# Products of 512 moving columns in the mLSTM (keys with values, gates of two heads) and in part of the last down projection, on one core

## The chip, the cores and the metric

The kernel runs on one core of a Trainium2 chip. The metric is the device time of one execution in microseconds (us). Engines are named as the profile names them: PE is TensorE's matmul (PEld its weight load), DVE is VectorE, ACT ScalarE, POOL GpSimd, SP the engine that issues most DMAs.

## The reference

A trunk of two layers runs over 640 tokens (512 of a prompt, 8 times 16 of a sample batch), model width 1024, all in 32-bit floats. In each layer one input projection feeds three mixers (a linear recurrence, an mLSTM with four heads of width 256, and windowed attention); their outputs are projected, gated, merged and projected again, and an MLP of width 4096 follows. What the change touches, cut to what matters:

```
u = rms_norm(x, norm1_g)
z = u @ w_in                     # (xa, ga, mq, mk, mv, mo, mi, mf, ...) = split(z)
k_m = mk * M_HEAD_DIM ** -0.5    # keys; q_m = mq, v_m = mv; 4 heads of 256 columns each
# per chunk: w = (q k^T) * exp(log_d - m_t);  num = w v + inter_w * (q C)
#            C_new = decay * C + sum_s wk_s k_s v_s^T     (C: 256 x 256 per head and sequence)
y_b = (rms_norm(h_m) * sigmoid(mo)) @ w_ob
...
x = x + square(relu(rms_norm(x, norm2_g) @ w_up)) @ w_down
```

The prompt is one sequence. The sample batch is eight sequences, each with its own stored C of 256 x 256 per head, which is read, used and written back.

## The kernel before

**Products.** Each 32-bit operand is split into a high part that TensorE takes in its fast 32-bit format (type fp32r) and a low rest. A product is three passes: high times high, low times high, high times low. Weights come in jobs of 1024 rows by 256 columns, in one fixed list (`jobs`). `prep` loads half a job into one of two raw buffers (`wraw`), casts the high part on ACT (L142) and subtracts on DVE for the low part (L143); a pair `whi`, `wlo` holds 256 rows, so that a job fills four pairs of six buffers each. `next_w` prepares one job ahead.

`gemm_w` (L167) holds the weights still and moves 320 token columns. `gemm_x` (L185) holds 128 tokens still and moves 256 weight columns: five blocks of tokens (t = 0 to 4) one after the other, each with 24 matmuls, so that a block's result leaves as soon as it is done, while the next is computed.

**Accumulators.** PSUM has eight banks of 512 floats a partition. `ps_acc` gives one of two tiles of two banks (`acc`), which only the big products use. `ps_small` gives one of four tiles of one bank (`psb`), which everything else shares.

**The mLSTM** (L408 and on). For each head the program writes down: keys by `gemm_x`, queries by `gemm_w`, values by `gemm_x`, output gates by `gemm_x`; transposes of the keys (L507, L510); then the head's recurrence over five blocks of tokens, each with scores (L538), a product with the values (L545), with the carried state (L548) and an update of it (L552). In the fifth block `sample` takes the eight stored states. For each sequence it loads C into one of five `cb` buffers (L451), splits it (`ch` on ACT L455, `cl` on DVE L456), multiplies it with the queries (L459, four matmuls that gather in one of two `psb` tiles kept for four sequences each), forms the update from `kvs` (L463, two matmuls, each into a `psb` tile), adds it on DVE (L465) and stores C (L467). The head ends with a chain of small DVE operations (L572 to L579), five scalings (L581) and ten transposes (L587, L590). While this goes on the block's own result (`pn`) keeps a third `psb` tile.

**What sets the order.** The engines take their instructions in the order of their own queues, and that order is fixed when the program is built. A scheduler chooses it by a simulation of its own: an instruction that stands earlier in the source goes first when its inputs and its buffer are there, and a later one fills in where it is not. So in the program before the products of the next head fill PE between the recurrence's steps. SP issues the DMAs in order too: where one waits for a buffer, those behind it wait.

**The last down projection** (L1179 to L1186) runs `gemm_x` four times with 256 output columns each and adds on DVE (L1181); the outputs leave by DMA.

## Time and profile before

| | us |
|---|---|
| median of three runs | 2929.08 (2927.71 to 2935.36) |
| profiled execution | 2926.99 |
| its span (first to last instruction) | 2925.1 |
| PE busy in it | 2881.9 (99%) |
| DVE, ACT, POOL busy | 1539.6, 1144.9, 304.2 |
| matmuls of `gemm_w`: 13440 of 320 columns (L167) | 1397.2 + 717.3 busy |
| matmuls of `gemm_x`: 4560 of 256 or 264 columns (L185) | 410.6 + 217.4 busy |

Busy time of PE counts a matmul from start to end, and matmuls overlap; how fast they follow each other is read from their starts in the timeline. The mLSTM of the two layers lies at 470 to 840 us and at 1930 to 2300 us of the span.

### The profile page before, as it was taken

To read this page: it belongs to the slowest core of one execution; us is meant where nothing else is said; L and a number is where in the kernel's file an instruction comes from. 1 tells how busy PE (TensorE), PEld (TensorE's weight loads), DVE (VectorE), ACT (ScalarE), POOL (GpSimd) and SP (SyncE) were. 2 spreads that over 40 slices of the span, in tenths; PEclk is the share of its full clock that TensorE was granted. 3 is DMA by queue.
4 is the path that set the end of the run, shared out by engine and by line. 5 is a ranking of instruction groups with operands and counts; after the bars stand their busy time and mean duration, and the time that the engine had idled before them with its cause. 6 is when DMAs were issued, how large, how long until landed. Compare 5 with 4: busy or idle time off the path is not lost.

```text
span 2925.1 us, 50762 instructions
## 1 busy us (share of the span) xinstructions
PE 2881.9 (99%) x20518; PEld 2849.7 (97%) x20518; DVE 1539.6 (53%) x3074; ACT 1144.9 (39%) x2295; POOL 304.2 (10%) x377
## 2 busy tenths in 40 slices
PE   8999999999999999999999999999999999999999
PEld 8999999999999999999999999999999999999999
DVE  7967675444553443333479666655454635333332
ACT  5754444333432332232358444433333323232222
POOL 0210000110112011010012100010111120110110
PEclk9999999999999999999999999999999999999999
DMA  5232224444573322222332322234444733222222
GB/s 172 68 118 80 78 81 118 142 132 134 158 262 108 109 74 83 75 72 73 104 88 68 117 83 80 89 110 146 138 148 139 250 119 100 73 73 73 80 79 73
DMA packets 291210, 319.52 MB, mean 109 GB/s; under 512 B 26424, under 2 KB 259688, under 8 KB 290944
## 3 DMA queue, kind: packets, MB, share of 16 engines
q1 hardware_dynamic: 281440, 300.03, 33.4%
q10 hardware_dynamic: 9536, 16.26, 1.5%
q8 instruction: 161, 2.64, 0.4%
q14 instruction: 73, 0.60, 0.1%
HBM read 255.76 MB, written 62.04 MB: 109 GB/s over the span
## 4 chain that ended last, share of the span: by engine, by line
PE 90%; DVE 4%; DMA 3%; ACT 2%; issue 1%; SPq 0%; POOL 0%; DVEq 0%; ACTq 0%; POOLq 0%
PE acc L167 63%; PE acc L185 16%; DMA out_C_s<-cb 2%; PE psb L743 2%; PE psb L713 1%; PE psb L552 1%; PE psb L735 1%; PE psb L1014 1%; PE psb L548 1%; DVE wlo L143 1%; DMA cb<-in_state_mlstm_C 1%; PE psb L459 1%; PE psb L538 1%; PE psb L545 1%; PE psb L803 0%
## 5 line engine op out<-in xcount | busy, mean ns | idle before, releaser
L167 PE MATMUL acc<-at,whi 128*128 128x320 f32 x8960 | 1397.2, 310 | 1.7 <-DVE xq L972 0.8
L167 PEld LDWEIGHTS acc<-at,whi 128*128 128x128 f32 x8960 | 1330.4, 188 | 3.9 <-issue 1.2
L167 PE MATMUL acc<-at,wlo 128*128 128x320 f32 x4480 | 717.3, 310 | 0.0
L167 PEld LDWEIGHTS acc<-at,wlo 128*128 128x128 f32 x4480 | 670.4, 188 | 0.8
L142 ACT CAST whi<-wraw 128x512 fp32r<-128x512 f32 (+1 forms) x712 | 425.8, 620 | 573.4 <-PE acc L167 496.9
L143 DVE TENSOR_TENSOR wlo<-wraw,whi 128x512 fp32r<-128x512 f32 (+1 forms) x712 | 468.9, 702 | 264.5 <-ACT whi L142 183.0
L185 PE MATMUL acc<-whi,at 128*128 128x256 f32 (+1 forms) x3040 | 410.6, 285 | 14.7 <-ACT vt L499 4.5
L185 PEld LDWEIGHTS acc<-whi,at 128*128 128x128 f32 x3040 | 380.5, 190 | 19.6 <-ACT vt L499 6.0
L185 PE MATMUL acc<-wlo,at 128*128 128x256 f32 (+1 forms) x1520 | 217.4, 282 | 0.0
L185 PEld LDWEIGHTS acc<-wlo,at 128*128 128x128 f32 x1520 | 196.0, 188 | 0.1
L1153 POOL TENSOR_TENSOR ha<-ha 128x640 f32<-128x640 f32 x64 | 82.0, 1281 | 824.4 <-DVE ha L1152 824.4
L1161 DVE TENSOR_TENSOR x<-x,acc 128x640 f32<-128x640 f32 x56 | 45.8, 818 | 153.2 <-PE acc L167 153.2
L116 DVE TENSOR_TENSOR at<-ha,at 128x640 fp32r<-128x640 f32 x64 | 52.8, 825 | 135.1 <-ACT at L115 135.1
L1151 ACT ACTIVATE ha<-acc 128x640 f32<-128x640 f32 x64 | 45.2, 706 | 188.6 <-PE acc L167 188.6
L1152 DVE TENSOR_TENSOR ha<-ha,rbc 128x640 f32<-128x640 f32 x64 | 52.8, 825 | 109.9 <-ACT ha L1151 109.9
L455 ACT CAST ch<-cb 128x516 fp32r<-128x516 f32 x64 | 39.6, 623 | 107.0 <-DMA cb<-in_state_mlstm_C 64.0
L115 ACT CAST at<-ha 128x640 fp32r<-128x640 f32 x64 | 46.6, 728 | 75.0 <-POOL ha L1153 74.3
L465 DVE SCALAR_TENSOR_TENSOR cb<-cb,decb,psb 128x258 f32<-128x258 f32 x128 | 58.1, 478 | 21.3 <-PE psb L463 21.1
L882 ACT ACTIVATE sg<-sg,cvh 128x640 f32<-128x640 f32 x48 | 40.0, 833 | 71.3 <-DVE sg L881 71.3
L691 ACT ACTIVATE prob<-psb,ssm 128x192 f32<-128x192 f32 (+2 forms) x128 | 49.6, 406 | 39.9 <-DVE ssm L689 39.9
L483 POOL TENSOR_SCALAR mo<-mo 128x256 f32<-128x256 f32 x40 | 39.3, 984 | 234.6 <-ACT mo L482 234.6
L456 DVE TENSOR_TENSOR cl<-cb,ch 128x516 fp32r<-128x516 f32 x64 | 43.8, 694 | 29.5 <-ACT ch L455 29.4
(332 smaller groups left out, 2587.3 us busy)
## 6 DMA issues: line engine op xcount, KB each, us to landing
wraw<-in_w_in SPq DMA_DIRECT2D x160, 512.0 KB
wraw<-in_w_up SPq DMA_DIRECT2D x64, 512.0 KB
wraw<-in_w_down SPq DMA_DIRECT2D x64, 512.0 KB
cb<-in_state_mlstm_C SPq DMA_DIRECT2D x64, 256.0 KB
out_C_s<-cb SPq DMA_DIRECT2D x64, 256.0 KB
gdr<-sg ACTq DMA_DIRECT2D x32, 320.0 KB
rl<-ydr SPq DMA_DIRECT2D x32, 320.0 KB
sg<-gdr SPq DMA_DIRECT2D x32, 320.0 KB
```

What stands on the lines that cost most here:

```text
L115: act.copy(dst[:, 0], src)
L116: dve.tensor_tensor(dst[:, 1], src, dst[:, 0].bitcast(F32), ALU.subtract)
L142: act.copy(hi[:, :, :n], r)
L143: dve.tensor_tensor(lo[:, :, :n], r, hi[:, :, :n].bitcast(F32), ALU.subtract)
L167: pe.matmul(acc[:, s, 0:320], lhs, xs[k][:, part, 320 * s:320 * s + 320], start=(i == 0 and k == 0 and part == 0), stop=(i == 1 and k == 7),)
L185: pe.matmul(o, xs[k][:, part, 128 * t:128 * t + 128], wt[:, k % KQ, 0:n], start=(i == 0 and k == 0 and part == 0), stop=(i == 1 and k == 7),)
L465: dve.scalar_tensor_tensor(cb[:, kt, :], cb[:, kt, :], decb[:, h, 4 + b:5 + b], ps[:, 0:258], op0=ALU.mult, op1=ALU.add)
L691: act.activation(o, s, AF.Exp, bias=nm[:, i:i + 1], accum_out=sums[:, i:i + 1])
L743: pe.matmul(po[:, 256 * i:256 * i + 256], vd[:, G - 1 + kb, g].rearrange("p a d -> p (a d)"), pTs[i][:, 256 * kb:256 * kb + 256], start=(k ...
L1152: dve.tensor_tensor(a, a, rbc, ALU.mult)
L1153: pool.tensor_tensor(a, a, a, ALU.mult)
L1161: dve.tensor_tensor(halves(xs[k]), halves(xs[k]), acc[:, :, 0:320], ALU.add)
```

## The change

Two jobs of 256 columns become one of 512, for the keys and values of each head, for the output gates of heads 0 and 1 and of heads 2 and 3, and for the first two of the four jobs of the last down projection. A new function `gemm_xw` computes such a job: it walks over the eight blocks of 128 weight rows, and within each over the five blocks of tokens, into five accumulators that all stay open to the end of the job. Four of them are the two `acc` tiles, the fifth is a `psb` tile. `prep` cuts such a job into four pieces of 256 rows, each loaded by two DMAs, and into eight pairs `whi`, `wlo` of 128 rows, which take turns in the same six buffers. The gates of two heads are computed with the first of them, and the values now directly with the keys.

```diff
@@ -132,6 +132,22 @@
     def prep(j, *hfs):
         ap, n = jobs[j]
         out = ready.setdefault(j, [])
+        if n == 512:
+
+            for q4 in range(4):
+                raw = wp.tile([128, 4, 264], F32, name="wraw", tag="wraw", bufs=2)
+                raw = raw.rearrange("p k c -> p (k c)")[:, 0:1024].rearrange("p (k c) -> p k c", k=2)
+                for i, a in enumerate(ap):
+                    wlast[0] = sp.dma_start(raw[:, :, 256 * i:256 * i + 256],
+                                            a[256 * q4:256 * q4 + 256, :].rearrange("(k p) c -> p k c", p=128))
+                for q in range(2):
+                    hi = wp.tile([128, KQ, 264], F32R, name="whi", tag="whi", bufs=6)
+                    lo = wp.tile([128, KQ, 264], F32R, name="wlo", tag="wlo", bufs=6)
+                    hi, lo = [w.rearrange("p k c -> p (k c)")[:, 0:512] for w in (hi, lo)]
+                    act.copy(hi, raw[:, q])
+                    dve.tensor_tensor(lo, raw[:, q], hi.bitcast(F32), ALU.subtract)
+                    out.append((hi, lo))
+            return
         for hf in hfs or (0, 1):
             raw = wp.tile([128, 4, 264], F32, name="wraw", tag="wraw", bufs=2)
             wlast[0] = sp.dma_start(raw[:, :, :n], ap[512 * hf:512 * hf + 512, :].rearrange("(k p) c -> p k c", p=128))
@@ -188,13 +204,32 @@
                         )
             evac(t, o)
 
+    def gemm_xw(xs, evac):
+
+        w = next_w()
+        a, b, c = ps_acc(), ps_acc(), ps_small()
+        os = [a[:, 0], a[:, 1], b[:, 0], b[:, 1], c]
+        for k in range(8):
+            for t in range(5):
+                x = [xs[k][:, part, 128 * t:128 * t + 128] for part in range(2)]
+                pe.matmul(os[t], x[1], w[k][0], start=(k == 0), stop=False)
+                pe.matmul(os[t], x[0], w[k][0], start=False, stop=False)
+                pe.matmul(os[t], x[0], w[k][1], start=False, stop=(k == 7))
+                if k == 7:
+                    evac(t, os[t])
+
     for l in range(depth):
         win = I["w_in"][l]
 
         def cols(c, n=256):
             return (win[:, c:c + n], n)
 
-        seq = [[cols(c + 256 * h) for c in (C_MK, C_MQ, C_MV, C_MO)] for h in range(4)]
+        def pair(a, b):
+            return ([win[:, a:a + 256], win[:, b:b + 256]], 512)
+
+        seq = [[pair(C_MK + 256 * h, C_MV + 256 * h), cols(C_MQ + 256 * h)] for h in range(4)]
+        for h in (0, 2):
+            seq[h].append(pair(C_MO + 256 * h, C_MO + 256 * h + 256))
         ga = [cols(C_G[0] + 256 * j) for j in range(4)]
         gb = [cols(C_G[1] + 256 * j) for j in range(4)]
         gc = [cols(C_G[2] + 256 * j) for j in range(4)]
@@ -216,7 +251,10 @@
         jobs += ow
         for g in range(4):
             jobs += [(I["w_up"][l][:, 1024 * g + 256 * j:1024 * g + 256 * j + 256], 256) for j in range(4)]
-            jobs += [(I["w_down"][l][1024 * g:1024 * g + 1024, 256 * j:256 * j + 256], 256) for j in range(4)]
+            dn = [(I["w_down"][l][1024 * g:1024 * g + 1024, 256 * j:256 * j + 256], 256) for j in range(4)]
+            if l == depth - 1 and g == 3:
+                dn[0:2] = [([dn[0][0], dn[1][0]], 512)]
+            jobs += dn
 
 
     ssum = [None]
@@ -475,31 +513,31 @@
 
         for h in range(4):
             ktok, qT, vt = wide("ktok", [128, 5, 256]), wide("qT", [128, 2, NT]), wide("vt", [128, 5, 258])
-            mo = wide("mo", [128, 5, 256])
+            if h % 2 == 0:
+                mos = [wide("mo", [128, 5, 256]) for _ in range(2)]
+            mo = mos[h % 2]
             kT, dd, qs = big("kT", [128, 2, NT], 1), big("dmat", [128, 5, 128], 1), big("qs", [128, 2, 384], 1)
 
             def ev_mo(t, o):
-                act.activation(mo[:, t, :], o, AF.Tanh, scale=rth[:, t:t + 1])
-                pool.tensor_scalar(mo[:, t, :], mo[:, t, :], 1.0, None, op0=ALU.add)
-
-
-            def ev_k(t, o):
-                act.activation(ktok[:, t, :], o, AF.Copy, scale=rt16[:, t:t + 1])
-
-            gemm_x(u, ev_k)
+                for i, mo_ in enumerate(mos):
+                    act.activation(mo_[:, t, :], o[:, 256 * i:256 * i + 256], AF.Tanh, scale=rth[:, t:t + 1])
+                    pool.tensor_scalar(mo_[:, t, :], mo_[:, t, :], 1.0, None, op0=ALU.add)
+
+            pool.memset(vt[:, :, 256:257], 1.0)
+            pool.memset(vt[:, :, 257:258], 0.0)
+
+            def ev_kv(t, o):
+                act.activation(ktok[:, t, :], o[:, 0:256], AF.Copy, scale=rt16[:, t:t + 1])
+                act.activation(vt[:, t, 0:256], o[:, 256:512], AF.Copy, scale=rtok[:, t:t + 1])
+
+            gemm_xw(u, ev_kv)
 
             def ev_q(m, acc):
                 dve.tensor_tensor(halves(qT[:, m, :]), acc[:, :, 0:320], halves(rbc), ALU.mult)
 
             gemm_w(u, ev_q)
-            pool.memset(vt[:, :, 256:257], 1.0)
-            pool.memset(vt[:, :, 257:258], 0.0)
-
-            def ev_v(t, o):
-                act.activation(vt[:, t, 0:256], o, AF.Copy, scale=rtok[:, t:t + 1])
-
-            gemm_x(u, ev_v)
-            gemm_x(u, ev_mo)
+            if h % 2 == 0:
+                gemm_xw(u, ev_mo)
 
             for kt in range(2):
                 ps = ps_small()
@@ -1177,13 +1215,13 @@
                     act.copy(yt[t][:, 512 * q4:512 * q4 + 512], ps)
 
             def ev_y(t, o):
-                c = slice(256 * j, 256 * j + 256)
+                c = slice(256 * j, 256 * j + (512 if j == 0 else 256))
                 dve.tensor_tensor(yt[t][:, c], yt[t][:, c], o, ALU.add)
                 dst = O["y_p"][0, 128 * t:128 * t + 128, c] if t < 4 else O["y_s"].rearrange("b s d -> (b s) d")[:, c]
                 sp.dma_start(dst, yt[t][:, c])
 
-            for j in range(4):
-                gemm_x(hid, ev_y)
+            for j in (0, 2, 3):
+                (gemm_x if j else gemm_xw)(hid, ev_y)
 
 
 
```

In the new program the lines behind 134 move: L459 becomes L497, L463 L501, L545 L583, L587 and L590 become L625 and L628, L465 L503, L451 L489, L467 L505; `gemm_xw` is L215 to L217.

PE where the sample part of head 0 begins in layer 0, the program before (`qm` are the queries, `ch` and `cl` the split state, `kvs` the operands of the update):

```order
L545 MATMUL psb<-vt,pt 128x257
L459 MATMUL psb<-ch,qm 128x258
L459 MATMUL psb<-cl,qm 128x258
L459 MATMUL psb<-ch,qm 128x258
L459 MATMUL psb<-cl,qm 128x258
L463 MATMUL psb<-kvs_5412 128x258 x2
L459 MATMUL psb<-ch,qm 128x258
L459 MATMUL psb<-cl,qm 128x258
L459 MATMUL psb<-ch,qm 128x258
L459 MATMUL psb<-cl,qm 128x258
L185 MATMUL acc<-whi,at 128x256 x16
L185 MATMUL acc<-wlo,at 128x256 x3
```

PE at the same place in the program after:

```order
L217 MATMUL acc<-wlo,at 128x512
L583 MATMUL psb<-vt,pt 128x257
L497 MATMUL psb<-ch,qm 128x258
L497 MATMUL psb<-cl,qm 128x258
L497 MATMUL psb<-ch,qm 128x258
L497 MATMUL psb<-cl,qm 128x258
L501 MATMUL psb<-kvs_5436 128x258 x2
L497 MATMUL psb<-ch,qm 128x258
L497 MATMUL psb<-cl,qm 128x258
L497 MATMUL psb<-ch,qm 128x258
L497 MATMUL psb<-cl,qm 128x258
L497 MATMUL psb<-ch,qm 128x258
```

Before, products of the next head stand between the eight sequences from the third on. After, the 48 matmuls of the sample part follow each other with none of the big products among them; the same holds for heads 0, 1 and 2 of both layers, and not for head 3, whose sample part has products of `gemm_w` in between.

PE where the same head ends, the program before (`num` is the head's result, transposed):

```order
L185 MATMUL acc<-whi,at 128x256 x9
L587 MATMUL psb<-cs,num 128x128
L185 MATMUL acc<-whi,at 128x256 x3
L587 MATMUL psb<-cs,num 128x128
L185 MATMUL acc<-whi,at 128x256 x2
L587 MATMUL psb<-cs,num 128x128
L185 MATMUL acc<-whi,at 128x256 x2
L185 MATMUL acc<-wlo,at 128x256
L587 MATMUL psb<-cs,num 128x128
```

PE at the same place in the program after:

```order
L497 MATMUL psb<-ch,qm 128x258
L497 MATMUL psb<-cl,qm 128x258
L501 MATMUL psb<-kvs_5437 128x258 x2
L625 MATMUL psb<-cs,num 128x128 x4
L628 MATMUL psb<-cs,num 128x128
L625 MATMUL psb<-cs,num 128x128 x4
L628 MATMUL psb<-cs,num 128x128
L215 MATMUL psb<-whi,at 128x512
L216 MATMUL psb<-whi,at 128x512
L217 MATMUL psb<-wlo,at 128x512
```

The ten transposes now follow the sample part directly. Behind them come the products of the fifth block of tokens of head 1's keys and values, which are the first to write the job's fifth accumulator (a `psb` tile): 72 of that job's 120 matmuls, those of the other four blocks of tokens for the first six blocks of weight rows, stand ahead of the sample part.

## Rows read from the trace of the kernel before

**Rows 1.** The page, busy time: engine, us (share of the span), instructions

```profile
PE 2881.9 (99%) x20518; PEld 2849.7 (97%) x20518; DVE 1539.6 (53%) x3074; ACT 1144.9 (39%) x2295; POOL 304.2 (10%) x377
```

**Rows 2.** Waits of PE over the span: us in total, times, longest

```profile
PE psb L587 <- DVE num L581: 5.2, 3, 3.6
PE acc L185 <- ACT vt L499: 4.5, 7, 2.0
...
PE psb L463 <- DVE cb L465: 3.5, 5, 1.1
PE acc L185 <- ACT ktok L487: 3.4, 2, 1.7
...
PE psb L459 <- ACT ch L455: 2.6, 4, 1.0
...
PE acc L185 <- DVE qT L492: 1.2, 3, 0.5
```

**Rows 3.** Timeline of PE, last down projection: start, us, engine, line, operation

```profile
2892.96 2.06 PE L185 MATMUL acc<-whi,at 128*128 128x256 f32 x16
2894.86 1.11 PE L185 MATMUL acc<-wlo,at 128*128 128x256 f32 x8
2895.80 2.05 PE L185 MATMUL acc<-whi,at 128*128 128x256 f32 x16
```

**Rows 4.** Timeline of PE, a stretch of `gemm_w`

```profile
888.76 4.85 PE L167 MATMUL acc<-at,whi 128*128 128x320 f32 x32
893.45 2.53 PE L167 MATMUL acc<-at,wlo 128*128 128x320 f32 x16
895.82 4.88 PE L167 MATMUL acc<-at,whi 128*128 128x320 f32 x32
```

**Rows 5.** Stretches from first L459 to last L590, heads 0 to 2, both layers

```profile
core 0: us, PE busy (x) PEld busy (x) DVE busy (x) ACT busy (x) POOL busy (x), PEclk, DMA share, GB/s
549.34:591.30 41.96, 40.09 (x305) 38.97 (x304) 28.62 (x81) 17.27 (x38) 3.67 (x10) 1.00 0.57 170
...
sum 244.34, PE 226.31 PEld 219.02 DVE 167.77 ACT 97.14 POOL 20.33; mean PE 37.72 PEld 36.50 DVE 27.96 ACT 16.19 POOL 3.39
```

**Rows 6.** Timeline of PE, sample part of head 0

```profile
549.77 0.28 PE L459 MATMUL psb<-ch,qm 128*128 128x258 f32 x1
549.88 0.28 PE L459 MATMUL psb<-cl,qm 128*128 128x258 f32 x1
550.00 0.40 PE L463 MATMUL psb<-kvs 128*128 128x258 f32 x2
550.24 0.28 PE L459 MATMUL psb<-ch,qm 128*128 128x258 f32 x1
```

**Rows 7.** DVE in 549.34 to 591.3: count, busy us, mean ns, idle before

```profile
L465 DVE SCALAR_TENSOR_TENSOR cb<-cb,decb,psb 128x258 f32<-128x258 f32 x16 | 7.2, 479 | 1.1 <-PE psb L463 1.1
...
L456 DVE TENSOR_TENSOR cl<-cb,ch 128x516 fp32r<-128x516 f32 x8 | 5.6, 696 | 1.4 <-ACT ch L455 1.4
L581 DVE SCALAR_TENSOR_TENSOR num<-num,fin,mo 128x256 f32<-128x256 f32 x5 | 2.1, 480 | 0.0
...
L452 DVE COPY cb<-nT 128x4 f32<-128x4 f32 x8 | 1.4, 169 | 7.8 <-DMA out_C_s<-cb 7.8
```

**Rows 8.** Timeline of SP: store of one state, next load into its buffer

```profile
552.36 0.39 SPq L467 DMA_DIRECT2D out_C_s<-cb  x1
555.55 0.38 SPq L451 DMA_DIRECT2D cb<-in_state_mlstm_C  x1
```

**Rows 9.** Timeline of ACT: the cast that waits for that load

```profile
558.74 0.62 ACT L455 CAST ch<-cb 128x516 fp32r<-128x516 f32 x1 [1.94 <-DMA cb<-in_state_mlstm_C]
```

**Rows 10.** Timeline of DVE: head 0's result begins, then its scalings

```profile
579.56 0.42 DVE L564 TENSOR_TENSOR num<-csum,psb 128x256 f32<-128x256 f32 x1
...
587.28 2.07 DVE L581 SCALAR_TENSOR_TENSOR num<-num,fin,mo 128x256 f32<-128x256 f32 x5
```

**Rows 11.** Timeline of PE: the last of head 0's transposes

```profile
591.02 0.27 PE L590 MATMUL psb<-cs,num 128*128 128x128 f32 x1
```

**Rows 12.** A stretch of layer 1 by engine, with the granted clock

```profile
2027.00:2031.00 4.00, 3.53 (x16) 3.33 (x17) 4.00 (x11) 1.58 (x5) 0.66 (x2) 0.58 0.49 105
```

**Rows 13.** Timeline of PE in that stretch

```profile
2027.68 3.68 PE L185 MATMUL acc<-whi,at 128*128 128x256 f32 x16 [0.47 <-DVE qT L492]
2031.19 0.75 PE L185 MATMUL acc<-wlo,at 128*128 128x256 f32 x5
```

**Rows 14.** ACT over layer 0's mLSTM: taking keys out of PSUM

```profile
L487 ACT ACTIVATE ktok<-acc,rt 128x256 f32<-128x256 f32 x20 | 9.2, 472 | 26.3 <-PE acc L185 26.2
```

## The prediction

> **What bounds the kernel now.** I read the page's busy times first: PE is busy for 2881.9 us of 2925.1 [rows 1], so 43 us are all that it ever waits, and every other engine has half its time free. Next come PE's waits: the largest are a few us each, and those inside the mLSTM's sample part (L587, L463, L459) make 5.2 + 3.5 + 2.6 = 11.3 us together, those at the ends of key, value and query jobs 4.5 + 3.4 + 1.2 = 9.1 us [rows 2]. So time can be gained only where PE needs less for the same work, and any wait of PE that is added is added to the whole. Last I read the timeline for what one product costs, and the order of the two programs for what stands beside the mLSTM's recurrence.
>
> **The products.** 3120 matmuls of 256 columns go: per layer 4 heads x 2 x 120 for keys and values and 4 x 120 for the gates, 1440, twice, and 240 of the down projection. 1560 of 512 columns come. Twenty-four of 256 columns follow each other in 2895.80 - 2892.96 = 2.84 us, 118.3 ns each [rows 3]; 48 of 320 columns in 7.06 us, 147.1 ns each [rows 4]. No matmul of 512 fp32r columns is in the trace. At the full clock of 2.4 GHz 256 more columns take 106.7 ns: 225.0 ns, a gain of 11.6 ns against two of 118.3, or 18 us in all. By the slope of the two rows (28.8 ns for 64 columns, 0.45 each) 512 take 233.5 ns: 3.1 ns a pair, 5 us in all. I take 7.7 ns, near the middle, 12 us.
>
> A sentence of the Trainium skill speaks for far more: "TensorE: Matmul & The Clock Gate", section "Back-to-back issue gap", gives about 131 ns a matmul at 512 columns in a stream of weight load and matmul pairs. By it a pair would save 2 x 118.3 - 131 = 105.6 ns, 165 us in all. The trace disagrees: 320 columns already take 147.1 ns [rows 4].
>
> **The place beside the recurrence.** This is the larger part. In the new order the products of the next head can't go on while a head's sample part runs. Their fifth accumulator is a `psb` tile, and all four of these are held by the recurrence, which stands earlier in the source. Without it no block of weight rows is finished, its buffers aren't given back, and after six of eight pairs (72 of 120 matmuls) there is nothing to multiply. So the 48 matmuls of the sample part and the ten transposes stand alone on PE, in six of eight heads. Before, PE was busy for 226.3 of 244.3 us in these six stretches [rows 5], mostly with big products. These products are not lost; they come afterwards, at full rate, and so each us that PE waits in such a stretch is added to the time.
>
> How long is a bare stretch? PE's own work in it: matmuls there follow each other at (550.24 - 549.77) / 4 = 0.12 us [rows 6], 58 of them, 7 us. The rest is the chain through DVE and the DMAs.
> - Upper bound: as long as with the products in between, 244.3 / 6 = 40.7 us, so 33.7 us idle.
> - Lower bound: DVE's own work for the chain. State updates 7.2, splits 5.6, scalings 2.1, copies 1.4 [rows 7], and, as an estimate, 5 for the mask, the sums and the small operations of the end (these and others filled the 7.7 us from 579.56 to 587.28 [rows 10]): 21 us, so 14 us idle.
> - Between them I follow the new order by hand, from the first state matmul at 0. The first update is done at 2.0. Its store takes 3.2 us until its buffer is free (552.36 to 555.55 [rows 8]), and a load as long until its cast can start (555.55 to 558.74 [rows 8, 9]). DVE does the second update only behind the next head's mask, whose load I let land at 3.5, and so the third at 7.2. Its buffer takes the eighth state: 7.2 + 3.2, about half a us in SP's queue, + 3.2 gives 14.1. Two casts of 0.62 and two splits of 0.70 (the seventh state comes just ahead) make 16. On DVE a small copy into the next head's buffer, which waits for the store of the sixth state, stands ahead of the last update, so that this ends at 19. From the first sum to the last transpose it took 591.29 - 579.56 = 11.7 us before [rows 10, 11]; with DVE free of weights and queries I take 10. That is 29 us, 22 idle.
> I take 22, nearer the lower bound, because in the rows of before DVE was also kept busy by weights (it was busy for 28.6 of 42 us [rows 5], and only 16.3 of them are in the four rows of [rows 7]). Six stretches: 132 us.
>
> **Smaller terms.** The clock: in 2027 to 2031 us the granted clock was 0.58, mostly the lower level of 1.2 GHz, after PE had waited several times within some us; sixteen matmuls took 3.51 us there from start to start [rows 12, 13], where 1.90 is usual [rows 3]. I add 1.5 us where the products start again after each bare stretch, 9 us; it could be nothing. In head 1 of each layer two steps of the recurrence also lose their products, which run out earlier: 3 us for four steps, bounded by 0 and 8. The waits of before that lie in the six stretches go, 10 of the 11.3 us above. At the ends of jobs five accumulators now fill together, and ACT needs 2 x 0.47 us for each [rows 14] against three matmuls, 0.7 us, on PE; on the other hand ten jobs end in a layer's mLSTM where sixteen did. I leave the 9.1 us as they are, with 0 to 24 as bounds (twelve such ends by the longest wait of 2.0 [rows 2]). Weights: as many bytes in twice as many DMAs of half the size, casts and splits as before, hidden by the products as now. In the last down projection the next jobs keep 256 columns, so the tail stays; of its first job the fifth accumulator is also a `psb` tile, but only the transposes of x use these there.
>
> **The sum.** 2926.99 (the profiled execution, 1.9 us more than its span) - 12 + 132 + 9 + 3 - 10 = 3050 us. The median of the runs is 2929.08, 0.07% above that execution; I leave 3050.
>
> **The rivals.**
> - The stretches shrink to DVE's own work: 14 us idle, 6 x 8 less, 3002 us. For it: DVE waits much for DMAs in before (7.8 us for stores alone [rows 7]), some of which SP's order causes. Against it: a store and a load still take 6.4 us, and three buffers turn over once.
> - They stay as long as before: 33.7 idle, 6 x 11.7 more, 3120 us. For it: the waits for DMAs don't depend on PE. Against it: DVE and SP lose the weights' work there.
> - Faster: the stretches cost next to nothing because the recurrence is ready each time that PE comes to it, and only the products' gain is left: 2926.99 - 12 = 2915 us. It decides from where a stretch idles for less than 12 / 6 = 2 us. For it: in before PE waited for the sample part only 11.3 us in eight heads [rows 2]. Against it: it did so because 30 us of other products stood between; DVE's own work alone is three times PE's.
> - Far faster, by a matmul of 512 columns in 131 ns: 3050 + 12 - 165 = 2897 us. That is the rule quoted above; rows 4 speak against it.
> - The change doesn't save on products at all (512 columns cost as much as two of 256): 3062 us, within the forecast's own range.
>
> **Chances.** The forecast, 3020 to 3085 us: 0.64. DVE's own work: 0.14. As long as before: 0.13. Some smaller loss, between 2938 and 2990: 0.03. Faster by the products alone 0.04, by the rule 0.01. That it ends within 0.3% of before, about what a measurement of this kernel can tell from no change, takes a balance of gain and waits that nothing favours: 0.01. So faster 0.05, same 0.01, slower 0.94. The range leaves out the far rivals: 3000 to 3105 us.
>
> **What the new profile would show.** Right: six stretches in which PE's busy share falls to a quarter or less, each 25 to 33 us from the first state matmul to the last transpose, with waits of PE's state and update matmuls (L497, L501) for DVE and of the transposes (L625) for the scalings; the clock at its lower level in them; PE idle for about 160 us in all; matmuls of 512 columns 225 to 234 ns apart; head 3 as before. Wrong: stretches as dense as before (then the reading of the order is wrong), or stretches of another length (then the chain by hand is). If the 512 columns come at 236 ns or more, the gain on products is nothing; if PE waits much at the ends of jobs, the term that I left unchanged is the one that failed.

## The result and the profile after

| | before | after |
|---|---|---|
| median of four runs, us | 2930.57 (2927.71 to 2935.36) | 3067.78 (3067.37 to 3069.2) |
| profiled execution, its span, us | 2926.99, 2925.1 | 3067.37, 3065.6 |
| mean granted clock of the span | 0.999 | 0.970 |

After is 1.0475 times before (95% interval 1.046 to 1.049), 137 us slower. The forecast was 3050 us, with a range of 3000 to 3105.

Busy time of the changed kernel, the line that answers to [rows 1]:

```profile
PE 2929.5 (96%) x18958; PEld 2801.3 (91%) x18958; DVE 1549.8 (51%) x3069; ACT 1146.3 (37%) x2295; POOL 293.3 (10%) x377
```

PE has 1560 matmuls less and is still busy 47.6 us longer. Span less busy time was 43.2 us and is 136.1. Busy time that grows while nothing is added is a sign of a lower clock, or of matmuls that stand apart and no longer overlap; the windows below show both.

What PE waited for, us in total, times, longest (answers to [rows 2]):

```profile
PE psb L625 <- DVE num L619: 51.9, 6, 9.3
PE psb L427 <- DVE dd L424: 18.1, 2, 9.0
PE psb L501 <- DVE cb L503: 10.9, 17, 1.4
PE psb L497 <- ACT ch L493: 9.6, 12, 1.6
PE psb L384 <- DVE gt L377: 9.2, 2, 4.6
PE psb L583 <- DVE pt L579: 4.2, 8, 0.7
```

Three groups of places. L625 are the heads' transposes, six times about 9 us; L501 and L497 are the sample parts. L384 and L427 are the gate stage of the mLSTM, once a layer; these waits are new and stand in no line of the forecast. Of the waits at the ends of key, value and query jobs, 9.1 us before, none is listed any more; 0.6 us of waits for keys taken out are left, at their transposes (L545).

The six stretches of [rows 5], heads 0 to 2 of both layers (us, busy time of each engine, granted clock, DMA):

```profile
584.70:614.22 29.52, 15.93 (x61) 11.53 (x60) 19.89 (x61) 8.73 (x20) 2.42 (x10) 0.62 0.57 171
...
sum 175.12, PE 95.53 PEld 69.90 DVE 118.18 ACT 52.80 POOL 17.66; mean PE 15.92 PEld 11.65 DVE 19.70 ACT 8.80 POOL 2.94
```

Before, the first stretch held 305 matmuls in 42 us; now it holds 61, its own 58 and the three at its edges, and the six last 28 to 31 us. They are 7 us of work at full clock and count 15.9 here. The granted clock falls to the lower level of 1.2 GHz inside the stretch, and a matmul that stands alone counts from start to end: 0.28 us in [rows 6], where such matmuls follow each other at 0.12.

Why nothing else stands there, by the groups of PE just before the stretch, 559 to 584.6 us (count behind the x):

```profile
L215 PE MATMUL acc<-whi,at 128*128 128x512 f32 x24 | 9.6, 400 | 0.0
L216 PE MATMUL acc<-whi,at 128*128 128x512 f32 x24 | 9.5, 395 | 0.0
L217 PE MATMUL acc<-wlo,at 128*128 128x512 f32 x24 | 9.4, 400 | 0.0
```

That is the next head's key and value job: 72 of 120 matmuls, all into `acc`, none into `psb`. The weights show the stop too. ACT's last cast of a weight ahead of the stretch and its next one are 57 us apart (timeline of ACT):

```profile
557.82 0.69 ACT L147 CAST whi<-wraw 128x512 fp32r<-128x512 f32 x1
...
615.11 0.62 ACT L147 CAST whi<-wraw 128x512 fp32r<-128x512 f32 x1
```

So the pairs of this job are not given back in between. Its first matmul into `psb` comes right behind the head's last transpose (timeline of PE: start, us):

```profile
601.20 0.63 PE L501 MATMUL psb<-kvs 128*128 128x258 f32 x2
611.10 1.66 PE L625 MATMUL psb<-cs,num 128*128 128x128 f32 x4 [9.27 <-DVE num L619]
...
613.80 0.42 PE L628 MATMUL psb<-cs,num 128*128 128x128 f32 x1
613.88 0.78 PE L215 MATMUL psb<-whi,at 128*128 128x512 f32 x1
614.45 0.63 PE L216 MATMUL psb<-whi,at 128*128 128x512 f32 x1
614.88 0.63 PE L217 MATMUL psb<-wlo,at 128*128 128x512 f32 x1
615.30 0.44 PE L215 MATMUL psb<-whi,at 128*128 128x512 f32 x1
```

The last rows also show the clock: from 613.88 on these matmuls start 0.42 to 0.57 us apart, where 0.23 is usual.

The gate stage of layer 0, the same view. Between 482.99 and 500.24 us PE has 14 short matmuls to do:

```profile
482.59 0.40 PE L217 MATMUL acc<-wlo,at 128*128 128x512 f32 x1
487.57 1.22 PE L384 MATMUL psb<-cs,gt 128*4 128x128 f32 x5 [4.58 <-DVE gt L377]
497.83 0.66 PE L427 MATMUL psb<-dd,ones 4*128 4x48 f32 x2 [9.04 <-DVE dd L424]
498.42 1.33 PE L432 MATMUL psb<-cs,pk 128*128 128x128 f32 x5
499.89 0.42 PE L457 MATMUL psb<-cs,nrow 32*128 32x32 f32 x2
500.24 0.80 PE L215 MATMUL psb<-whi,at 128*128 128x512 f32 x1
```

It is the same picture: head 0's own key and value job has stopped, and its first `psb` matmul comes behind the last matmul of the stage.

The 512-column matmuls themselves (answers to [rows 3]):

```profile
461.45 0.39 PE L217 MATMUL acc<-wlo,at 128*128 128x512 f32 x1
461.68 0.40 PE L215 MATMUL acc<-whi,at 128*128 128x512 f32 x1
```

Over the span the median is 231 ns from start to start. Two of 256 columns took 236.6 ns [rows 3], so a pair saves 5.6 ns and 1560 of them 8.7 us.

### The profile page after: what moved, and what is told of

It is laid out like the page before. It is cut to its first block, busy times and chain, and to the rows that moved or that the text cites. A ratio compares the mean times of both kernels' runs of the same rounds, so it can differ in the third digit from the quotient of the medians.

```text
span 3065.6 us, 47823 instructions
## 1 busy us (share of the span) xinstructions
PE 2929.5 (96%) x18958; PEld 2801.3 (91%) x18958; DVE 1549.8 (51%) x3069; ACT 1146.3 (37%) x2295; POOL 293.3 (10%) x377
## 4 chain that ended last, share of the span: by engine, by line
PE 74%; DMA 4%; DVE 3%; ACT 1%; issue 1%; SPq 0%; POOL 0%; ACTq 0%; DVEq 0%; POOLq 0%
PE acc L183 53%; PE acc L201 3%; PE acc L215 3%; PE acc L216 3%; PE acc L217 3%; DMA out_C_s<-cb 1%; DMA cb<-in_state_mlstm_C 1%; PE psb L590 1%; PE psb L215 1%; PE psb L216 1%; PE psb L781 1%; PE psb L217 1%; PE psb L586 1%; PE psb L583 1%; PE psb L625 1%
## 5 line engine op out<-in xcount | busy, mean ns | idle before, releaser
L158 ACT CAST whi<-wraw 128x512 fp32r<-128x512 f32 (+1 forms) x608 | 370.0, 622 | 578.6 <-PE acc L183 509.1
L159 DVE TENSOR_TENSOR wlo<-wraw,whi 128x512 fp32r<-128x512 f32 (+1 forms) x608 | 404.5, 703 | 232.1 <-ACT whi L158 150.1
L215 PE MATMUL acc<-whi,at 128*128 128x512 f32 x416 | 166.3, 400 | 0.1
L216 PE MATMUL acc<-whi,at 128*128 128x512 f32 x416 | 164.1, 395 | 0.0
L217 PE MATMUL acc<-wlo,at 128*128 128x512 f32 x416 | 162.0, 394 | 0.0
L148 DVE TENSOR_TENSOR wlo<-wraw,whi 128x512 fp32r<-128x512 f32 x104 | 70.9, 699 | 126.0 <-ACT whi L147 92.0
L201 PE MATMUL acc<-whi,at 128*128 128x256 f32 (+1 forms) x960 | 127.5, 283 | 5.8 <-DVE sg L919 3.1
L201 PEld LDWEIGHTS acc<-whi,at 128*128 128x128 f32 x960 | 119.0, 188 | 8.1 <-DVE sg L919 3.9
L147 ACT CAST whi<-wraw 128x512 fp32r<-128x512 f32 x104 | 65.1, 626 | 141.8 <-PE acc L183 56.9
L215 PEld LDWEIGHTS acc<-whi,at 128*128 128x128 f32 x416 | 78.2, 188 | 18.1 <-ACT vt L531 1.6
L217 PEld LDWEIGHTS acc<-wlo,at 128*128 128x128 f32 x416 | 78.2, 188 | 17.3
L216 PEld LDWEIGHTS acc<-whi,at 128*128 128x128 f32 x416 | 78.2, 188 | 15.9
```

The costliest lines, as they stand in the source:

```text
L147: act.copy(hi, raw[:, q])
L148: dve.tensor_tensor(lo, raw[:, q], hi.bitcast(F32), ALU.subtract)
L158: act.copy(hi[:, :, :n], r)
L159: dve.tensor_tensor(lo[:, :, :n], r, hi[:, :, :n].bitcast(F32), ALU.subtract)
L201: pe.matmul(o, xs[k][:, part, 128 * t:128 * t + 128], wt[:, k % KQ, 0:n], start=(i == 0 and k == 0 and part == 0), stop=(i == 1 and k == 7),)
L215: pe.matmul(os[t], x[1], w[k][0], start=(k == 0), stop=False)
```

## The experiments

Theory: the fifth accumulator of a row-block job is a `psb` tile; while gate stage or recurrence holds these, the job stops, its weights stay in their buffers, and PE has no other work. Rivals: the width of 512 columns or the row-block form costs wherever it stands; eight weight pairs in six buffers hold PE up; the length of a stretch is a matter of the buffers of stored states. Each run has its own runs of before on the same chip (2927.8 to 2930.6 us).

### Head 0's keys and values at 256 columns

```diff
-seq = [[pair(C_MK + 256 * h, C_MV + 256 * h), cols(C_MQ + 256 * h)] for h in range(4)]
+seq = [[cols(c + 256 * h) for c in (C_MK, C_MQ, C_MV)] if h == 0 else
+       [pair(C_MK + 256 * h, C_MV + 256 * h), cols(C_MQ + 256 * h)] for h in range(4)]
-            gemm_xw(u, ev_kv)            # and head 0: gemm_x(u, ev_k) ... gemm_x(u, ev_v)
```

> Head 0's keys and values go back to two jobs of 256 columns; heads 1 to 3, the gates and the down projection stay at 512. Theory (starved accumulator: while the recurrence or the gate stage of the mLSTM holds all `psb` tiles, a row-block job can't start its fifth accumulator, gives no weights back and so PE has nothing else to do): the two bare stretches at the gate stages (layer 0 near 483 to 500 us, layer 1 near 2005 to 2022 us, 27 us of waits at L384 and L427 and some 6 us of half clock) fill with products again, the six bare stretches of the sample parts stay: 3067.8 - 33 + 240 x 5.6 ns = about 3036 us, and the waits L384 and L427 on DVE fall below 2 us. Rival (those waits belong to the gate stage itself, products of head 0 only happened to stand there before): no change, 3069 us. Rival (what costs is the 512-column form of a job, wherever it stands): 2 of 13 jobs less, 3067.8 - 137 x 2/13 = about 3047 us, spread over the program and not at the gate stages.

Measured: 3036.93 us, ratio 1.037 (1.0352 to 1.0387), 30.9 us below the changed kernel. No wait for `gt` or `dd` is listed any more, and the transposes wait as before:

```profile
PE psb L637 <- DVE num L631: 51.4, 6, 9.9
```

So the gate stages cost 32 us (30.9, and 1.3 that head 0's 240 matmuls of 512 columns no longer save), and it is head 0's job that leaves them bare. The rivals' 3069 and 3047 are out.

### Keys and values in row blocks of 256 columns, in the kernel before

```diff
+    def gemm_xn(xs, evac):                       # as gemm_xw, 256 columns, pairs of 256 rows
+        a, b, c = ps_acc(), ps_acc(), ps_small()
+        os = [a[:, 0, 0:256], a[:, 1, 0:256], b[:, 0, 0:256], b[:, 1, 0:256], c[:, 0:256]]
...
-            gemm_x(u, ev_k); gemm_w(u, ev_q); gemm_x(u, ev_v)
+            gemm_xn(u, ev_k); gemm_xn(u, ev_v); gemm_w(u, ev_q)
```

> The kernel before with 256 columns everywhere, but keys and values each computed row block by row block into five accumulators, the fifth a `psb` tile, keys then values then queries; gates and down projection as before. A job's four weight pairs fit in the six buffers. In its order the sample parts of heads 0 to 2 hold 54 products of 256 columns (6.4 us) in their first half, then 26 matmuls and the ten transposes stand bare. Theory (starved accumulator): no 512-column job is left, and yet most of the loss is there: 6 x (22 - 6.4) = 94 us, 2930.6 + 94 = about 3025 us (2995 to 3045), with PE waiting for DVE at the transposes as in the changed kernel. Rival (width of 512 columns): 2925 to 2940 us. Rival (eight weight pairs in six buffers): 2925 to 2940 us, as four pairs fit.

Measured: 3031.8 us, 1.035 (1.0334 to 1.0365). There is no 512-column matmul in it and a job's weights fit in the buffers, yet three quarters of the loss are there. (The values also stand ahead of the queries here, as in the changed kernel; the run with four accumulators below keeps that order and has no such loss.) Its six stretches together, by engine:

```profile
sum 180.60, PE 111.25 PEld 94.38 DVE 123.86 ACT 58.88 POOL 12.75; mean PE 18.54 PEld 15.73 DVE 20.64 ACT 9.81 POOL 2.13
```

The end of the first one, timeline of PE:

```profile
588.93 1.67 PE L601 MATMUL psb<-cs,num 128*128 128x128 f32 x4 [7.87 <-DVE num L595]
...
591.63 0.42 PE L604 MATMUL psb<-cs,num 128*128 128x128 f32 x1
591.70 0.56 PE L198 MATMUL psb<-whi,at 128*128 128x256 f32 x1
```

Of 180.6 us, 6 x (7 + 54 x 0.118) = 80 are work at full clock; 100 are lost, and 15 in the gate stages (PE waits 15.2 us for `dd`). Less the 11 us of waits that lay in these places before, that is 104; the run is 102 us slower than before. Again the first matmul into `psb` follows the last transpose. Width and weight buffers are not needed for the loss. By the count the buffers add to it in the changed kernel: with eight pairs held a job could do 96 matmuls ahead of the stretch and not 72. That is argued, as no version with eight pairs was tried.

### Gates and down projection alone; down projection alone

The first is the changed kernel with keys, queries and values as before (the condition of the first diff true for all heads); the second is the kernel before with only the last down projection's first two jobs joined.

> The changed kernel with keys and values of every head as two jobs of 256 columns again, in the order of before; the gates of two heads and the first two jobs of the last down projection stay at 512 (600 of 1560 matmuls). In its order all stretches beside the recurrence hold products, and the row-block jobs of the gates lie beside the recurrence's first steps. Theory (what costs is the starved fifth accumulator beside gate stage and sample part): the loss goes and 600 x 5.6 ns = 3.4 us of gain stay: 2926 us (2920 to 2938). Rival (each 512-column job costs the same wherever it is): 2929 + 137 x 5/13 = about 2982 us.

> The kernel before with only the first two jobs of the last down projection joined to 512 columns (120 matmuls instead of 240); the mLSTM as before. No recurrence stands beside this job. Theory (the form costs nothing by itself): 120 x 5.6 ns = 0.7 us less, no difference that can be measured: 2927 to 2932 us, 512-column matmuls 231 ns from start to start, and PE waiting under 1 us where this job ends. Rival (five accumulators that fill together hold PE up at the end of each such job): 137 / 13 = 10 us more for this one job, 2940 us, with a wait of PE for DVE's additions at L1181's place.

Measured: 2926.78 us against 2930.04, 0.9995 (0.9984 to 1.0005), and 2927.68 against 2927.78, 1.0002 (0.9993 to 1.0011). Neither can be told from before. The medians lie 3.3 and 0.1 us below before, where 3.4 and 0.7 were expected, but neither gain is shown by such intervals. What is shown: 600 of the 1560 matmuls, in the same form and with the same buffers, cost nothing that can be measured where they stand. The loss belongs to keys and values. In the first, PE's waits at the transposes are down from 51.9 us to 3.6.

### Queries first

```diff
-seq = [[pair(C_MK + 256 * h, C_MV + 256 * h), cols(C_MQ + 256 * h)] for h in range(4)]
+seq = [[cols(C_MQ + 256 * h), pair(C_MK + 256 * h, C_MV + 256 * h)] for h in range(4)]
-            gemm_xw(u, ev_kv); gemm_w(u, ev_q)
+            gemm_w(u, ev_q); gemm_xw(u, ev_kv)
```

> The changed kernel with each head's queries (256 columns by `gemm_w`, which uses only `acc` tiles) ahead of its keys and values instead of behind them; all 512-column jobs stay. In its order the gate stages of head 0 are filled, and in the sample parts of heads 0 and 2 stand some 72 matmuls of 512 columns, 16.6 us of work by 231 ns each; head 1's sample part has only four, and the ends of the heads (ten transposes) stay bare. Theory (starved accumulator beside the recurrence): 33 us come back at the gate stages and 4 stretches x 15 us = 60: 3067.8 - 93 = about 2975 us (2955 to 3000), with the two head 1 stretches as long and bare as before. Rival (the six weight buffers can't hold a job of eight pairs, PE waits for weights): the jobs are the same, 3060 to 3070 us. Rival (512-column form costs wherever it stands): the same, 3060 to 3070 us.

Measured: 3014.75 us, 1.029 (1.0274 to 1.0305): 53 us back of the 93 expected. The four stretches that now hold 72 products, by engine:

```profile
sum 150.40, PE 110.03 PEld 88.83 DVE 89.85 ACT 36.51 POOL 9.65; mean PE 27.51 PEld 22.21 DVE 22.46 ACT 9.13 POOL 2.41
```

PE's new waits in it, us in total, times, longest:

```profile
PE acc L183 <- DVE sg L958: 7.2, 2, 3.8
PE acc L215 <- DVE qT L534: 6.2, 2, 3.1
...
PE acc L215 <- ACT vt L531: 3.0, 2, 1.6
```

They are 37.6 us long on average, where the same four (heads 0 and 2) took 28.6 in the changed kernel: the products lengthen a stretch by 9.0 of their own 16.6 us. So 30 us come back in four stretches and 32 at the gate stages, and 14 go into the new waits (2.3 of `sg` were there already). That makes 48 of the 53; the rest is not assigned. My expectation counted filler as if a stretch kept its length; it doesn't.

### Six buffers for the stored states

`bufs=5` of `cb` becomes 6 in the changed kernel; PE's order there stays.

> The changed kernel with six instead of five buffers `cb` for the stored states; the order on PE up to head 3 is the same, the bare stretches stay bare. It asks what sets the length of a bare stretch. If it is the turn of the buffers (store of a state, load of the next; in the stretch of head 0 ACT waits 4.6, 2.4, 2.7 and 1.0 us for such loads): each stretch loses one turn of three, some 3 us of 29.5, and the time falls by 6 x 3 to about 3050 us (3040 to 3062). If it is DVE's own chain (updates, splits, 24 small operations of the end): stretches stay at 28 to 31 us and the time at 3066 to 3069 us.

Measured: 3066.46 us, 1.0468 (1.0453 to 1.0484), as the changed kernel. The six stretches are 174.2 us, by 0.9 shorter. So one buffer more, which the expectation made worth 3 us a stretch, is worth 0.15. The end of the first stretch on DVE, in the changed kernel:

```profile
601.62 0.17 DVE L490 COPY cb<-nT 128x4 f32<-128x4 f32 x1 [0.50 <-DMA out_C_s<-cb]
602.94 0.17 DVE L490 COPY cb<-nT 128x4 f32<-128x4 f32 x1 [1.14 <-DMA out_C_s<-cb]
603.07 0.70 DVE L494 TENSOR_TENSOR cl<-cb,ch 128x516 fp32r<-128x516 f32 x1
603.68 0.87 DVE L503 SCALAR_TENSOR_TENSOR cb<-cb,decb,psb 128x258 f32<-128x258 f32 x2
604.58 0.43 DVE L512 TENSOR_TENSOR csum<-csum,psb 64x258 f32<-64x258 f32 x1
...
610.56 2.07 DVE L619 SCALAR_TENSOR_TENSOR num<-num,fin,mo 128x256 f32<-128x256 f32 x5
```

PE is done with the states at 601.8. Ahead of the last update and sum DVE has two copies and a split for the next head's states, and the copies wait for stores. From 604.6 to 610.6 it runs 24 operations one after the other, most of them small ones of the head's end, then the scalings. With six buffers four such copies wait 3.1 us in the first stretch (2.7 with five), for other stores. The chain that ended last, followed back through the same place of that run, still goes through two stores (start, us):

```profile
599.23 3.87 DMA out_C_s<-cb
...
603.67 3.12 DMA out_C_s<-cb
```

Of that chain from 594 to 616 us the stores are 47% with six buffers and 48% with five. So waiting for stores has not left the chain; beside it stands DVE's own work at the end. Which of these would have to go for a shorter stretch was not tried, and what sets the length stays open.

### A bank of its own, and its control

```diff
-        a, b, c = ps_acc(), ps_acc(), ps_small()
+        a, b, c = ps_acc(), ps_acc(), psC.tile([128, 512], F32, name="psc", tag="psc")
-    psB = ctx.enter_context(tc.tile_pool(name="psB", bufs=4, space=PSUM))
+    psB = ctx.enter_context(tc.tile_pool(name="psB", bufs=3, space=PSUM))
+    psC = ctx.enter_context(tc.tile_pool(name="psC", bufs=1, space=PSUM))
```

The control is the kernel before with `bufs=3` for `psB` and nothing else.

> The changed kernel with one of the four `psb` tiles taken out of the pool and given to the row-block jobs as their fifth accumulator (pool `psC`, one tile; `psb` has three). Width, order in the source and the six weight buffers stay as in the changed kernel. In its order products stand in all gate stages and in the sample parts of heads 0 to 2; bare are the end of head 3 (25 state matmuls and nine transposes), and at head 3's start 36 matmuls of the recurrence in a row. Theory (starved accumulator): nearly all of the 137 us comes back; what stays is what three `psb` tiles cost the recurrence, which the kernel before with three tiles measures by itself, less 8.7 us for the products: 2930 to 2965 us, I take 2945. Rival (six buffers for eight weight pairs, or the 512-column form itself): above 3030 us, with PE idle for over 100 us.

> The kernel before with three `psb` tiles instead of four, all jobs of 256 columns: the price of the bank alone. Its order fills the sample parts of heads 0 to 2 as before; 25 state matmuls and nine transposes at head 3's end and 36 matmuls of the recurrence ahead of it stand bare, twice. By the lengths of such bare pieces in the changed kernel (transposes' wait 9, half of a sample part 6) I take 2 x 12 = 24 us: 2929.3 + 24 = about 2953 us (2932 to 2975). The run with an own bank should then lie 8.7 us below this one (5 to 14), 1560 matmuls by 5.6 ns; under the rival (the form of the job costs) it lies far above.

> The run with queries first and the run with an own bank put together: all jobs of 512 columns, an own fifth accumulator, queries ahead of keys and values. In its order products stand in the gate stages, in all sample parts and between the transposes of heads 0 to 2; head 3's end stays bare, as with three `psb` tiles in every order. Theory: as the own bank alone, less what its bare 12 and 17 matmuls of the recurrence cost: 2925 to 2955 us, and if the queries' first place again lets PE wait for the evacuations of keys, values and queries (12 us in the run with queries first), no better than the own bank alone. Rival (form or weight buffers): above 3000 us.

Measured: own bank 3062.49 us, 1.0461 (1.0447 to 1.0475); the control 3059.28, 1.0447 (1.0433 to 1.0461); own bank with queries first 3070.98, 1.0494 (1.0478 to 1.051). All expected times were missed; queries first is no better than the own bank alone, as its expectation allowed. The six stretches with an own bank, by engine:

```profile
sum 289.00, PE 269.34 PEld 241.26 DVE 172.99 ACT 118.43 POOL 15.41; mean PE 44.89 PEld 40.21 DVE 28.83 ACT 19.74 POOL 2.57
```

Of the largest waits of PE in the control, those of the attention:

```profile
PE psb L735 <- ACT qp L841: 17.7, 5, 3.9
...
PE psb L735 <- DVE prob L696: 12.0, 4, 3.7
PE psb L793 <- DVE sprob L696: 10.1, 4, 2.6
```

The own bank fills the stretches (269 of 289 us busy), and PE has no wait for `gt` or `dd` any more. But the fourth `psb` tile is worth 129 us to the kernel before: with three the attention (L735, L793) waits too, outside the mLSTM. I had priced it at 24 by looking at the mLSTM alone. Against its control the changed kernel with an own bank is 3 us slower instead of 137, which agrees with the theory, though the products' 8.7 us of gain don't show; as a proof it is weak, since the control moved as far as the change did.

### Four accumulators, the fifth block of tokens as a second pass

```diff
+    def gemm_x4(xs, evac):
+        w = next_w()
+        a, b = ps_acc(), ps_acc()
+        os = [a[:, 0], a[:, 1], b[:, 0], b[:, 1]]
+        for ts in ((0, 1, 2, 3), (4,)):
+            if ts == (4,):
+                w = next_w()
+                os.append(ps_acc()[:, 0])
...
-            gemm_xw(u, ev_kv)
+            gemm_x4(u, ev_kv)          # seq: the pair of keys and values stands twice
```

A second version has queries first, a third the gates of each head as a job of 256 columns again (`gemm_x(u, ev_mo)` in each head).

> The changed kernel with all 512-column products kept and `psb` at four tiles, but keys and values no longer open a fifth accumulator: the first four blocks of tokens go row block by row block into the two `acc` tiles, and the fifth block follows as a pass of its own (24 matmuls of 512 columns) into an `acc` tile, with the same weights loaded, cast and split a second time. Matmuls on PE are as many as in the changed kernel; ACT and DVE split 8 jobs x 8 pairs once more, 128 x 512 each, by 0.6 to 0.7 us some 5 us a job on each, and the DMAs load 16.8 MB more. In its order products stand in all gate stages and sample parts; bare are ten transposes at the end of head 1. Theory (starved `psb` accumulator): all of the loss goes and the products' gain is seen: 2930 - 1560 x 5.6 ns = 2921, plus up to 9 for each bare end of head 1: 2921 to 2940 us, I take 2928. Rival (512-column form, bursts of results, or eight pairs in six buffers): these are all still there, above 3030 us. Rival (the doubled weights overload DVE and ACT beside the recurrence): 2945 to 2990 us, with PE waiting for L493, L494 and for weights.

> The same, with each head's queries ahead of its keys and values. It asks whether the order of the jobs matters once no job needs a `psb` tile beside the recurrence. Theory: as the run with four accumulators, within 10 us of it (2921 to 2940 us); the waits of PE for the taking out of queries and values (12 us with queries first in the changed kernel) may come with it. Rival (form or weight buffers): above 3030 us.

> The run with four accumulators and, besides, the output gates of each head as a job of 256 columns of their own, as before. Keys and values stay at 512 columns, row block by row block, four blocks of tokens into the two `acc` tiles and the fifth as a second pass; of the last down projection the first two jobs stay joined. 1080 matmuls of 512 columns are left (8 x 120 and 120). In its order no sample part, no gate stage and no end of a head stands bare: the gates' job is back beside each head's end, where the run with four accumulators had ten bare transposes in head 1 (16.7 us of waits at the scalings in six heads and resumption at a lower clock). Theory (the loss is whatever stands bare on PE, and nothing in the 512-column form): 33 us of the run with four accumulators go, and 1080 x 5.6 ns = 6 us of gain stay: 2929 - 6 = 2923 us (2918 to 2936), with PE's idle time back near 40 us. Rival (the doubled casts and splits of keys and values load DVE and ACT beside the recurrence): as the run with four accumulators, 2950 to 2965 us, with PE waiting for the splits and for `cb`.

Measured: 2960.62 us, 1.011 (1.0094 to 1.0125); 2975.66, 1.0163 (1.0149 to 1.0177); 2966.42, 1.0124 (1.0107 to 1.0141). In the first, with `psb` at four tiles, the same 1560 matmuls of 512 columns, the same order of jobs and no `psb` accumulator for keys and values, 107 of 137 us are back: the theory's main test holds, the rivals' 3030 and more are out. The rest was expected wrongly. With queries first PE waits 21.4 us for `sg` and 6.2 for the queries, and the run is 15 us slower than the first. What was left of the first's loss I put down to bare ends of heads; the third version waits for the scalings only 4.0 us, where the first waits 16.7, and is no faster. Among the largest waits of PE there:

```profile
PE psb L515 <- ACT ch L511: 9.3, 5, 3.6
PE acc L201 <- ACT mo L540: 9.0, 6, 2.9
PE psb L519 <- DVE cb L521: 6.3, 6, 2.0
```

Its busy times by engine:

```profile
PE 2893.4 (98%) x19438; PEld 2810.2 (95%) x19438; DVE 1575.7 (53%) x3133; ACT 1178.2 (40%) x2359; POOL 299.0 (10%) x377
```

PE waits for ACT and DVE at many places. That speaks for the rival of that expectation: the second casts and splits (64 more on each than in the changed kernel, 32 us on ACT and 26 on DVE) come where these engines have the recurrence to serve. How much of the first version's 33 us is this and how much its bare ends stays open: no run has the bare ends without the second preparation.

No version is shown to be faster than the kernel before. Keys and values apart is the best, 4.6% faster than the changed kernel and not to be told from before.

## Why the prediction was right, and where it was off

The sign and the reason held; 3068 lies 18 us above 3050 and within the range. By its own steps:

- **What bounds the kernel.** Right: each us that PE waits was added. Gain on products, losses and vanished waits make up the difference of the two executions (sum below).
- **The products, -12.** The saving is 5.6 ns a pair, not 7.7: -8.7. The 131 ns a matmul of the Trainium skill ("TensorE: Matmul & The Clock Gate", section "Back-to-back issue gap") are not what fp32r operands do here: 231 ns were measured.
- **The place beside the recurrence, +132.** Right in place, number and size: six stretches of 28.0 to 30.9 us, 175.1 - 6 x 7 = 133. The mechanism is what the first two runs and the four accumulators show. The length, 29 us by hand and 29.2 measured, was right partly by luck: the stores and the copy that waits for one ahead of the last update are there, but a sixth buffer, which should have saved a turn, saved 0.15 us a stretch.
- **PE idle for about 160 us.** 136 by the page. The matmuls in the stretches, at half speed or standing alone, count as busy: PE's busy share there is 55% (15.9 of 29.2 us), where the forecast's own sign was a quarter or less.
- **The clock at resumption, +9.** 0.6 to 1.6 us each, 6 in all. Behind the first stretch three matmuls took 1.42 us from 613.88 on, where 0.69 is usual, and then the pace is nearly back; behind the third eight took 3.42, where 1.85 is usual.
- **Head 1's two steps, +3.** PE waits 4.2 us in eight steps for `pt` (L583).
- **Waits of before that vanish, -10.** Right: the 11.3 us lay in stretches that now are something else.
- **Ends of jobs, 0.** Off: 9.1 us became 0.6, a gain of 8.5, where the bounds, 0 to 24 us of waiting, were drawn mostly for a loss.
- **Left out: the gate stages, +32.** This is the step that was missing. The reading "the products can't go on while a head's sample part runs" is true of every stage that holds `psb` tiles, and the prediction applied it to the sample parts alone. Head 0's keys and values stand beside the gate stage as those of heads 1 to 3 stand beside a recurrence. The head 0 run shows 32 us.

Sum with what was measured: -8.7 + 133 + 6 + 4 - 11 - 8.5 + 32 = 147; the two executions differ by 140.4. The 6 to 7 us between are not assigned.

## What to carry to other kernels

Before making a product hold more accumulators at once, list each stage that draws on the same pool, also those of other parts of the program that run beside it, and ask of each whether the product can go on without the tile. On an engine that is busy for 99% filler is as valuable as work: a gain of 5.6 ns a matmul, 8.7 us in all, cost 165 us of filler. And price a buffer by a run with one less before giving it away: a look at one stage gave 24 us where the kernel lost 129.

## What the hardware did that I had not expected

Matmuls of fp32r follow each other at 118.3, 147.1 and 231 ns for 256, 320 and 512 columns: from 320 on 0.437 ns a column, near the 0.417 of 2.4 GHz, so that wider ones have little left to save. In the bare pieces the granted clock falls to its lower level of 1.2 GHz, after PE had done short pieces of work between waits; the gate stage of layer 0, where it falls within the window, and the end of the first stretch, all at the lower level (us, busy times of PE, PEld, DVE, ACT and POOL, then the granted clock, DMA share and GB/s):

```profile
482.60:500.20 17.60, 3.83 (x16) 2.21 (x14) 13.13 (x44) 3.23 (x7) 0.00 (x0) 0.59 0.15 37
...
591.50:615.40 23.90, 12.38 (x39) 8.97 (x40) 14.40 (x49) 6.17 (x13) 1.04 (x8) 0.50 0.56 171
```

The products that follow pay 0.6 to 1.6 us for it behind each of the six stretches, and 1.3 and 2.0 us behind the two gate stages.
